# Moving the start addresses of the matmul operands of a two-layer decoder trunk

## The chip, the cores and the metric
The kernel runs on one core of a Trainium2 chip. The metric is device time in microseconds, the median of three runs; the profiler adds one profiled execution, whose span goes from its first to its last instruction.

## The reference
The program computes a decoder trunk of two layers for 256 tokens of 2048 features in float32. Layer 0 mixes tokens with a sparse attention of three branches, layer 1 with a matrix memory (mLSTM); after each mixer stands a gated feed-forward network with a short convolution. All large products have the form `xn @ w`:

```
x = x + nsa_mixer(rms_norm(x, g0), ...)          # xn @ w_in (2048 x 3632), o @ w_out (2048 x 2048)
x = x + conv_glu_ffn(rms_norm(x, g1), ...)       # u = xn @ w_up (2048 x 11264); conv; silu(gate)*val @ w_down (5632 x 2048)
x = x + mlstm_mixer(rms_norm(x, g2), ...)        # xn @ w_in (2048 x 6160), h @ w_out (2048 x 2048)
x = x + conv_glu_ffn(rms_norm(x, g3), ...)
return rms_norm(x, norm_final)
```

## The kernel before, in words
Precision comes from splitting. Every operand is held as a high half, rounded to the format `float32r` that TensorE takes, and a low half, the rest; a product is three matmuls into one PSUM bank: high by high, high by low, low by high. The activations are `xh` and `xl`, laid out with features on the partitions. Weights come from memory as `raw` (SyncE's queue, 512 KB a piece, four buffers); ACT copies `raw` to `whi` (line 189), DVE subtracts to `wlo` (line 191), five buffers each; TensorE then takes them.

A matmul has a stationary operand, which a weight load (PEld) brings in, and a moving operand, which is streamed. There are two forms.

The columns form (`cols_piece`, lines 225 to 228) is used for the attention's compressed keys and values, keys and queries, for the mLSTM's queries and keys and for the whole up projections. The weights are stationary (128 x 128), the 256 tokens of `xh` or `xl` are moving. A piece is 4 feature tiles x 2 column tiles x 3 matmuls = 24 matmuls; the three are (whi, xh), (whi, xl), (wlo, xh), stationary operand first.

The rows form (`rows_mm`, lines 197 to 199) has the activations stationary and the weights moving. Its order is (high, whi), (high, wlo), (low, whi). It serves two uses: the projections of `xh`/`xl` that are wanted with tokens on partitions (`rows_times`, 256 to 512 columns), and all output projections (`project_out`, 512 columns and in the very last two banks 256), where the stationary operand is a stage's own output: `oh`/`ol` in the attention, `moh`/`mol` in the mLSTM, `gh`/`gl` in the feed-forward network.

The order of the work is the order in which the program issues it: side work (attention, mLSTM heads, norms) is handed out between pieces from a queue (`tick`), and evacuations of PSUM banks follow each product.

Tiles are placed one behind the other within a pool, and pools one behind the other, in the order of allocation. What a tile takes on each partition is its number of elements times 4 bytes, rounded up to 32. Added up from the start, that gives each tile's start address; its remainder modulo 256 is called its phase here. All large tiles are multiples of 256 bytes long, as are the steps between buffers, feature tiles and 128-column blocks, so a phase holds for every buffer and nearly every block of a tile; the exceptions are the widths 412, 416 and 304 of `rows_times`, whose second and third blocks begin inside a tile at another phase. Unused pad tiles (`pad_w`, `pad_x`, `pad_m`, `pad_f`) set the phases. Before, they are: `xh` and `xl` 96; `raw`, `whi`, `wlo` 32; `gh`, `gl`, `oh`, `ol`, `moh`, `mol` 32.

Of the kernel before, what the change touches and what calls it, by code (L numbers as in the profile page):

```python
# [12 lines left out]
F32 = mybir.dt.float32  # L13
# [8 lines left out]
P = 128  # L22
# [40 lines left out]
def trunk(ctx: ExitStack, tc: tile.TileContext, x, positions, nsa_w_in, nsa_gate_b, nsa_cmp_pe,  # L63
# [8 lines left out]
    const = ctx.enter_context(tc.tile_pool(name="const", bufs=1))  # L72
    main = ctx.enter_context(tc.tile_pool(name="main", bufs=1))
    wpool = ctx.enter_context(tc.tile_pool(name="wpool", bufs=1))
    wpool.tile([P, 48], F32, name="pad_w")
    small = ctx.enter_context(tc.tile_pool(name="small", bufs=2))
    psum = ctx.enter_context(tc.tile_pool(name="psum", bufs=8, space=PSUM))

# [2 lines left out]
    def nm(s):  # L81
        uid[0] += 1
        return f"{s}_{uid[0]}"
# [4 lines left out]
    def fview(t):  # L88
        return t.bitcast(F32)

    h = main.tile([P, NT, D], F32, name="h")
    main.tile([P, 16], F32, name="pad_x")
    xh = main.tile([P, KT, S], F32R, name="xh")
    xl = main.tile([P, KT, S], F32R, name="xl")

# [75 lines left out]
    def queued(engine):  # L171
        return tc.issue_after(fence[engine]) if engine in fence else nullcontext()
# [3 lines left out]
    def preload(w, k0, nk, c0, n):  # L176
        ready[w.tensor.name, w.offset, k0, c0] = load_split(w, k0, nk, c0, n)

    def load_split(w, k0, nk, c0, n):
        got = ready.pop((w.tensor.name, w.offset, k0, c0), None)  # L180
        if got is not None:
            return got
        view = lambda t: t[:, :nk * n].rearrange("p (k c) -> p k c", k=nk)
        raw = wpool.tile([P, 1024], F32, name=nm("raw"), tag="raw", bufs=RAWB)
        nc.sync.dma_start(view(raw), w[k0 * P:(k0 + nk) * P, c0:c0 + n].rearrange("(k p) c -> p k c", p=P))
        hi = wpool.tile([P, 1024], F32R, name=nm("whi"), tag="whi", bufs=SPB)
        lo = wpool.tile([P, 1024], F32R, name=nm("wlo"), tag="wlo", bufs=SPB)
        with queued("act"):
            latest["act"] = act(view(hi), view(raw), AF.Copy).ins  # L189
        with queued("ve"):  # L190
            latest["ve"] = ve.tensor_sub(view(lo), view(raw), fview(view(hi))).ins  # L191
        return view(hi), view(lo)
# [8 lines left out]
    def rows_times(w, c0, n, nk):  # L201
        accs = [bank() for _ in range(NT)]
        for k0 in range(0, KT, nk):
            m = min(nk, KT - k0)
            hi, lo = load_split(w, k0, m, c0, n)
            run_hooks()
            for i in range(m):
                kt = k0 + i
                for t in range(NT):
                    rows_mm(hi, lo, i, xh, xl, kt, t, accs[t][:, :n], 0, n, kt == 0, kt == KT - 1)  # L210
            tick()
        return accs
# [4 lines left out]
    def cols_piece(ps, w, c0, k0, n):  # L217
        hi, lo = load_split(w, k0, n, c0, 256)
        run_hooks()
        for i in range(n):  # L220
            for j in range(2):
                kt = k0 + i
                a = hi[:, i, j * P:(j + 1) * P]
                b = lo[:, i, j * P:(j + 1) * P]
                mm(ps[:, j, :], a, xh[:, kt, :], start=(kt == 0 and j == 0), stop=False,  # L225
                   skip_group_check=True)
                mm(ps[:, j, :], a, xl[:, kt, :], start=False, stop=False, skip_group_check=True)  # L227
                mm(ps[:, j, :], b, xh[:, kt, :], start=False, stop=(kt == KT - 1 and j == 1),  # L228
                   skip_group_check=True)
        tick()  # L230

    def cols_times(w, c0):
        ps = pair_bank()
        for k0 in range(0, KT, 4):
            cols_piece(ps, w, c0, k0, 4)
        return ps
# [109 lines left out]
    def nsa(norm, nxt):  # L346
        with tc.tile_pool(name="nsa", bufs=1) as pool, tc.tile_pool(name="nsw", bufs=2) as wk:
# [18 lines left out]
            pct = pool.tile([80, 512], F32R, name="pct")  # L366
            nc.gpsimd.memset(fview(vcmp), 0.0)
            nc.gpsimd.memset(fview(pct), 0.0)
            oh = pool.tile([P, HEADS, S], F32R, name="oh")
            ol = pool.tile([P, HEADS, S], F32R, name="ol")  # L370

            nc.gpsimd.dma_start(per, nsa_cmp_pe[0].rearrange("c l d -> l c d"))
# [303 lines left out]
    def mlstm(norm, nxt):  # L676
        with tc.tile_pool(name="mls", bufs=1) as pool, tc.tile_pool(name="mlw", bufs=2) as wk:
# [4 lines left out]
            sog = pool.tile([P, NT, D], F32, name="sog")  # L682
            v1 = pool.tile([P, NT, MH, DV + 1], F32, name="v1")
            nc.gpsimd.memset(v1[:, :, :, DV:DV + 1], 1.0)
            pool.tile([P, 16], F32, name="pad_m")
            oh = pool.tile([P, KT, S], F32R, name="moh")
            ol = pool.tile([P, KT, S], F32R, name="mol")
            gp = pool.tile([P, NT, 2 * MH], F32, name="gp")
            li, lf, u, w1p, bcol, ecol = (pool.tile([P, NT, MH], F32, name=n)
# [163 lines left out]

    def ffn(layer, norm, nxt):
        with tc.tile_pool(name=f"ffn{layer}", bufs=1) as pool, tc.tile_pool(name=f"ffw{layer}", bufs=2) as wk:
            pool.tile([P, 48], F32, name=f"pad_f{layer}")
            wu, wd = ffn_w_up[layer], ffn_w_down[layer]
            taps = tapc[:, layer]

            def conv(ff, tag, ps):  # L860
                uu = wk.tile([P, 2, S], F32, name=nm("u"), tag="u" + tag)
                ve.tensor_mul(uu, ps, norm.rbc2)  # L862
                ac = wk.tile([P, 2, S], F32, name=nm("ac"), tag="ac" + tag)
                for j in range(2):
                    f = ff + j
                    act(ac[:, j, :], uu[:, j, :], AF.Identity, bias=taps[:, 3, f:f + 1],  # L866
                        scale=taps[:, 2, f:f + 1])
                    ve.scalar_tensor_tensor(ac[:, j, 1:], uu[:, j, :S - 1], taps[:, 1, f:f + 1],  # L868
                                            ac[:, j, 1:], op0=ALU.mult, op1=ALU.add)
                    ve.scalar_tensor_tensor(ac[:, j, 2:], uu[:, j, :S - 2], taps[:, 0, f:f + 1],  # L870
                                            ac[:, j, 2:], op0=ALU.mult, op1=ALU.add)
                return ac

            groups = [list(range(0, 4))] + [list(range(f, f + 8)) for f in range(4, NFF, 8)]

            def up(ffs):
                gh = wk.tile([P, 8, S], F32R, name=nm("gh"), tag="gh")
                gl = wk.tile([P, 8, S], F32R, name=nm("gl"), tag="gl")
                for i in range(0, len(ffs), 2):
                    res = {}  # L880

                    def gate_out(ff, ps, res):
                        res["g"] = conv(ff, "g", ps)
                        act(res["g"], res["g"], AF.Silu)

                    def val_out(ff, ps, res, i):
                        va = conv(NFF + ff, "v", ps)
                        ve.tensor_mul(va, res["g"], va)
                        act(gh[:, i:i + 2, :], va, AF.Copy)
                        ve.tensor_sub(gl[:, i:i + 2, :], va, fview(gh[:, i:i + 2, :]))  # L890

                    evacs.append(partial(gate_out, ffs[i], cols_times(wu, ffs[i] * P), res))
                    evacs.append(partial(val_out, ffs[i], cols_times(wu, (NFF + ffs[i]) * P), res, i))
                return gh, gl

            def down(ffs, g, norm):
                n = len(ffs)
                project_out(wd[ffs[0] * P:(ffs[0] + n) * P, :], g[0], g[1], n, norm)

            prev = None  # L900
            for ffs in groups:
                g = up(ffs)
                if prev is not None:
                    down(*prev, None)
                prev = (ffs, g)
            down(*prev, nxt)
# [60 lines left out]
    after(8, partial(measure, 1))  # L967
    after(12, n0.settle)
    nsa(n0, n1)
    ffn(0, n1, n2)  # L970
    mlstm(n2, n3)
    nf.load()
    ffn(1, n3, nf)


# [21 lines left out]
```

## Time and profile before

| | us |
|---|---|
| median of 3 runs | 2221.46 (2220.2 to 2222.11) |
| the profiled execution's own time | 2222.36 |
| span of the profiled execution | 2220.6 |
| TensorE busy (99%) | 2203.8 |
| DVE busy (65%) | 1444.2 |
| ACT busy (50%) | 1113.4 |

A busy time is the sum of the stretches in which an engine has an instruction under way; matmuls overlap each other, so a matmul's own duration is longer than the distance to the next one. The distance is read from starts: in the timeline, or in the view of one source line, which gives a line's first and last start and how many there are. PE is TensorE's matmuls, PEld its weight loads. Names after `<-` are the operands.

### The profile page before, as it was taken

The page shows a single profiled execution, that of the slowest core. Times are in us where ns is not written, and L with a number is a line of the kernel's source. Part 1 is how long each engine was busy: PE and PEld are TensorE (multiplying, and loading weights), DVE is VectorE, ACT ScalarE, POOL GpSimd, SP SyncE. Part 2 cuts the span into 40 slices and gives each one's busy share as a digit, 9 for nine tenths or more (in the row PEclk, how much of TensorE's full clock was granted, in tenths as well). Part 3 has the DMA queues.
Part 4 walks back from the last instruction along what each step waited for, and adds up shares of the span by engine and source line. Part 5 has one row for each costly group of instructions (what it writes and reads, how often), then busy time and mean ns, then how long its engine had stood idle before and what let it go on. Part 6 is the DMA issues. An engine that isn't in the chain of part 4 may idle for free.

```text
span 2220.6 us, 37284 instructions
## 1 busy us (share of the span) xinstructions
PE 2203.8 (99%) x15072; PEld 2042.1 (92%) x15072; DVE 1444.2 (65%) x2191; ACT 1113.4 (50%) x1565; POOL 19.1 (1%) x56
## 2 busy tenths in 40 slices
PE   9999999999999999999999999999999999999998
PEld 8899789999999899998899988899999899998987
DVE  6488757676656666665645665667666566675755
ACT  6366655554445454454654444555545454454544
POOL 2000000000000000000000000000000000000000
PEclk9999999999999999999999999999999999999999
DMA  8653355666666666666567655566666666666664
GB/s 242 204 166 106 112 162 180 189 183 190 188 191 189 191 187 186 192 187 191 165 187 200 171 171 167 169 197 191 188 191 184 193 185 189 190 187 192 184 195 133
DMA packets 298317, 403.33 MB, mean 182 GB/s; under 512 B 12904, under 2 KB 256840, under 8 KB 298016
## 3 DMA queue, kind: packets, MB, share of 16 engines
q1 hardware_dynamic: 297264, 399.03, 59.6%
q8 instruction: 118, 1.93, 0.4%
q0 software_dynamic: 688, 1.83, 0.3%
q14 instruction: 55, 0.45, 0.1%
q10 hardware_dynamic: 192, 0.08, 0.0%
HBM read 398.80 MB, written 2.10 MB: 181 GB/s over the span
## 4 chain that ended last, share of the span: by engine, by line
PE 97%; DMA 1%; ACT 1%; DVE 1%; issue 0%; SPq 0%; ACTq 0%
PE bank L225 18%; PE bank L228 18%; PE bank L227 18%; PE bank L197 13%; PE bank L199 13%; PE bank L198 13%; DMA raw<-in_nsa_w_in_dram 1%; PE bank L548 1%; PE bank L259 1%; PE bank L579 0%; DMA h<-in_x_dram 0%; ACT whi L189 0%; ACT pr L552 0%; PE bank L523 0%; DVE wlo L191 0%; PE bank L597 0%
## 5 line engine op out<-in xcount | busy, mean ns | idle before, releaser
L191 DVE TENSOR_TENSOR wlo<-raw,whi 128x1024 fp32r<-128x1024 f32 (+3 forms) x755 | 912.6, 1210 | 609.8 <-ACT whi L189 607.4
L189 ACT ACTIVATE whi<-raw 128x1024 fp32r<-128x1024 f32 (+3 forms) x755 | 790.4, 1048 | 955.3 <-PE bank L227 483.5
L225 PE MATMUL bank<-xh,whi 128*128 128x256 f32 x3456 | 970.4, 281 | 3.2 <-ACT whi L189 2.6
L228 PE MATMUL bank<-xh,wlo 128*128 128x256 f32 x3456 | 965.8, 280 | 1.5 <-DVE wlo L191 1.5
L227 PE MATMUL bank<-xl,whi 128*128 128x256 f32 x3456 | 965.4, 279 | 0.1
L225 PEld LDWEIGHTS bank<-xh,whi 128*128 128x128 f32 x3456 | 649.1, 188 | 7.7 <-ACT whi L189 3.4
L228 PEld LDWEIGHTS bank<-xh,wlo 128*128 128x128 f32 x3456 | 650.1, 188 | 1.9 <-DVE wlo L191 1.9
L227 PEld LDWEIGHTS bank<-xl,whi 128*128 128x128 f32 x3456 | 648.2, 188 | 1.3 <-DVE xl L265 0.4
L197 PE MATMUL bank<-whi,gh 128*128 128x512 f32 (+1 forms) x712 | 276.1, 388 | 0.0
L199 PE MATMUL bank<-whi,gl 128*128 128x512 f32 (+1 forms) x712 | 275.5, 387 | 0.0
L198 PE MATMUL bank<-wlo,gh 128*128 128x512 f32 (+1 forms) x712 | 275.3, 387 | 0.0
L199 PEld LDWEIGHTS bank<-whi,gl 128*128 128x128 f32 x712 | 133.7, 188 | 27.4
L198 PEld LDWEIGHTS bank<-wlo,gh 128*128 128x128 f32 x712 | 133.8, 188 | 26.8
L197 PEld LDWEIGHTS bank<-whi,gh 128*128 128x128 f32 x712 | 133.7, 188 | 26.5
L197 PE MATMUL bank<-whi,xh 128*128 128x412 f32 (+4 forms) x352 | 128.0, 364 | 0.0
L199 PE MATMUL bank<-whi,xl 128*128 128x412 f32 (+4 forms) x352 | 125.2, 356 | 0.0
L198 PE MATMUL bank<-wlo,xh 128*128 128x412 f32 (+4 forms) x352 | 125.1, 355 | 0.0
L866 ACT ACTIVATE ac<-u,tapc 128x256 f32<-128x256 f32 x176 | 95.0, 587 | 3.8 <-DVE u L862 3.8
L310 DVE TENSOR_TENSOR h<-bank,h 128x512 f32<-128x512 f32 (+1 forms) x113 | 72.9, 682 | 34.5 <-PE bank L199 34.3
L862 DVE TENSOR_TENSOR u<-bank,rbc 128x512 f32<-128x512 f32 x88 | 60.8, 691 | 52.8 <-PE bank L228 52.8
L868 DVE SCALAR_TENSOR_TENSOR ac<-u,tapc,ac 128x255 f32<-128x255 f32 x176 | 77.3, 479 | 3.0 <-ACT ac L866 3.0
L870 DVE SCALAR_TENSOR_TENSOR ac<-u,tapc,ac 128x254 f32<-128x254 f32 x176 | 77.2, 479 | 0.3
(251 smaller groups left out, 1505.6 us busy)
## 6 DMA issues: line engine op xcount, KB each, us to landing
raw<-in_ffn_w_up_dram SPq DMA_DIRECT2D x352, 512.0 KB, 3.7
raw<-in_ffn_w_down_dram SPq DMA_DIRECT2D x176, 512.0 KB, 4.4
raw<-in_mlstm_w_in_dram SPq DMA_DIRECT2D x64, 512.0 KB, 3.8
raw<-in_nsa_w_in_dram SPq DMA_DIRECT2D x51, 512.0 KB, 4.6
raw<-in_nsa_w_out_dram SPq DMA_DIRECT2D x32, 512.0 KB, 3.7
raw<-in_mlstm_w_out_dram SPq DMA_DIRECT2D x32, 512.0 KB, 4.4
raw<-in_mlstm_w_in_dram SPq DMA_DIRECT2D x32, 412.0 KB, 4.1
raw<-in_nsa_cmp_w_dram SPq DMA_DIRECT2D x16, 256.0 KB, 3.4
```

The lines of the kernel that those rows point to most:

```text
L189: latest["act"] = act(view(hi), view(raw), AF.Copy).ins
L191: latest["ve"] = ve.tensor_sub(view(lo), view(raw), fview(view(hi))).ins
L197: mm(o, a, hi[:, i, c:e], start=first, stop=False)
L198: mm(o, a, lo[:, i, c:e], start=False, stop=False)
L199: mm(o, b, hi[:, i, c:e], start=False, stop=last)
L225: mm(ps[:, j, :], a, xh[:, kt, :], start=(kt == 0 and j == 0), stop=False, skip_group_check=True)
L227: mm(ps[:, j, :], a, xl[:, kt, :], start=False, stop=False, skip_group_check=True)
L228: mm(ps[:, j, :], b, xh[:, kt, :], start=False, stop=(kt == KT - 1 and j == 1), skip_group_check=True)
L310: ve.tensor_add(h[:, t, a:b], acc[:, :b - a], h[:, t, a:b])
L866: act(ac[:, j, :], uu[:, j, :], AF.Identity, bias=taps[:, 3, f:f + 1], scale=taps[:, 2, f:f + 1])
L868: ve.scalar_tensor_tensor(ac[:, j, 1:], uu[:, j, :S - 1], taps[:, 1, f:f + 1], ac[:, j, 1:], op0=ALU.mult, op1=ALU.add)
L870: ve.scalar_tensor_tensor(ac[:, j, 2:], uu[:, j, :S - 2], taps[:, 0, f:f + 1], ac[:, j, 2:], op0=ALU.mult, op1=ALU.add)
```

## The change
The change touches pad tiles alone: two are made smaller, one larger, one is taken away and five are added. `pad_w` goes from 48 to 16 words and `pad_x` goes; a pad of 32 words (128 bytes) is put between the `whi` and the `wlo` buffers, before `oh` and before `ol`, between `moh` and `mol`, and between the `gh` and the `gl` buffers; `pad_m` grows from 16 to 48 words and `pad_f` shrinks from 48 to 16. No instruction, operand shape, order or buffer count is altered. Added up in the same way, the phases become:

| tiles | before | after |
|---|---|---|
| xh, xl | 96 | 32 |
| raw, whi | 32 | 96 |
| wlo | 32 | 224 |
| gh, oh, moh | 32 | 96 |
| gl, ol, mol | 32 | 224 |

```diff
-    wpool.tile([P, 48], F32, name="pad_w")
+    wpool.tile([P, 16], F32, name="pad_w")
...
-    main.tile([P, 16], F32, name="pad_x")
...
+    apart = []
+
     def load_split(w, k0, nk, c0, n):
...
         hi = wpool.tile([P, 1024], F32R, name=nm("whi"), tag="whi", bufs=SPB)
+        if not apart:
+            apart.append(wpool.tile([P, 32], F32, name="pad_lo"))
         lo = wpool.tile([P, 1024], F32R, name=nm("wlo"), tag="wlo", bufs=SPB)
...
+            pool.tile([P, 32], F32, name="pad_oh")
             oh = pool.tile([P, HEADS, S], F32R, name="oh")
+            pool.tile([P, 32], F32, name="pad_ol")
             ol = pool.tile([P, HEADS, S], F32R, name="ol")
...
-            pool.tile([P, 16], F32, name="pad_m")
+            pool.tile([P, 48], F32, name="pad_m")
             oh = pool.tile([P, KT, S], F32R, name="moh")
+            pool.tile([P, 32], F32, name="pad_n")
             ol = pool.tile([P, KT, S], F32R, name="mol")
...
-            pool.tile([P, 48], F32, name=f"pad_f{layer}")
+            pool.tile([P, 16], F32, name=f"pad_f{layer}")
+            pads = []
...
                 gh = wk.tile([P, 8, S], F32R, name=nm("gh"), tag="gh")
+                if not pads:
+                    pads.append(wk.tile([P, 32], F32, name=f"pad_g{layer}", tag="pad_g", bufs=1))
                 gl = wk.tile([P, 8, S], F32R, name=nm("gl"), tag="gl")
```

## Rows read from the trace of the kernel before

**Rows 1.** The page, busy shares and 40 slices: TensorE and its granted clock in tenths.
```profile
PE 2203.8 (99%) x15072; PEld 2042.1 (92%) x15072; DVE 1444.2 (65%) x2191; ACT 1113.4 (50%) x1565; POOL 19.1 (1%) x56
...
PE   9999999999999999999999999999999999999998
...
PEclk9999999999999999999999999999999999999999
```
**Rows 2.** The page's chain by engine and line; then TensorE's waits, us, times, longest.
```profile
PE 97%; DMA 1%; ACT 1%; DVE 1%; issue 0%; SPq 0%; ACTq 0%
PE bank L225 18%; PE bank L228 18%; PE bank L227 18%; PE bank L197 13%; PE bank L199 13%; PE bank L198 13%; DMA raw<-in_nsa_w_in_dram 1%; PE bank L548 1%; PE bank L259 1%; PE bank L579 0%; DMA h<-in_x_dram 0%; ACT whi L189 0%; ACT pr L552 0
...
PE bank L225 <- ACT whi L189: 2.6, 2, 1.8
PE bank L228 <- DVE wlo L191: 1.5, 2, 0.8
```
**Rows 3.** Timeline, up projection of layer 0: start us, us, engine, line, operands.
```profile
699.87 0.28 PE L225 MATMUL bank<-xh,whi 128*128 128x256 f32 x1
699.87 0.19 PEld L227 LDWEIGHTS bank<-xl,whi 128*128 128x128 f32 x1
699.99 0.28 PE L227 MATMUL bank<-xl,whi 128*128 128x256 f32 x1
```
**Rows 4.** Groups by line and shape, TensorE: xcount | busy us, mean ns | idle before.
```profile
L225 PE MATMUL bank<-xh,whi 128*128 128x256 f32 x3456 | 970.4, 281 | 3.2 <-ACT whi L189 2.6 <-ACT xh L264 0.6
...
L197 PE MATMUL bank<-whi,gh 128*128 128x512 f32 x696 | 271.6, 390 | 0.0
...
L197 PE MATMUL bank<-whi,xh 128*128 128x512 f32 x128 | 52.7, 411 | 0.0
L197 PE MATMUL bank<-whi,moh 128*128 128x512 f32 x128 | 51.2, 400 | 0.0
L197 PE MATMUL bank<-whi,oh 128*128 128x512 f32 x128 | 51.0, 399 | 0.0
...
L197 PE MATMUL bank<-whi,xh 128*128 128x412 f32 x128 | 44.5, 348 | 0.0
```
**Rows 5.** Line 225 in one up projection: count, durations, first and last start.
```profile
L225 PE MATMUL bank<-xh,whi x256: 280/280/282, 640.2 to 730.3; 128*128 128x256 f32 x128
```
**Rows 6.** Line 197 in one down projection, in the same form.
```profile
L197 PE MATMUL bank<-whi,gh x64: 389/389/402, 864.6 to 907.5; 128*128 128x512 f32 x64
```
**Rows 7.** Timeline, one query piece during the attention; 21 starts lie between.
```profile
166.54 0.28 PE L227 MATMUL bank<-xl,whi 128*128 128x256 f32 x1
...
168.92 0.28 PE L227 MATMUL bank<-xl,whi 128*128 128x256 f32 x1
```
**Rows 8.** Timeline, NSA value columns, xh stationary; 20, then 14 starts apart.
```profile
37.84 0.28 PE L197 MATMUL bank<-whi,xh 128*128 128x256 f32 x1
...
40.19 0.28 PE L199 MATMUL bank<-whi,xl 128*128 128x256 f32 x1
...
44.41 0.28 PE L197 MATMUL bank<-whi,xh 128*128 128x256 f32 x1
...
46.00 0.28 PE L199 MATMUL bank<-whi,xl 128*128 128x256 f32 x1
```
**Rows 9.** Timeline, end of the last down projection, 256 columns; 24 starts apart.
```profile
2208.56 0.28 PE L199 MATMUL bank<-whi,gl 128*128 128x256 f32 x1
...
2211.44 0.28 PE L199 MATMUL bank<-whi,gl 128*128 128x256 f32 x1
```
**Rows 10.** Timeline, mLSTM value columns, xh stationary, 512 columns; 12 starts apart.
```profile
1228.22 0.39 PE L197 MATMUL bank<-whi,xh 128*128 128x512 f32 x1
...
1231.02 0.39 PE L197 MATMUL bank<-whi,xh 128*128 128x512 f32 x1
```
**Rows 11.** The page's costliest groups, DVE and ACT: busy, mean ns | idle, releaser.
```profile
L191 DVE TENSOR_TENSOR wlo<-raw,whi 128x1024 fp32r<-128x1024 f32 (+3 forms) x755 | 912.6, 1210 | 609.8 <-ACT whi L189 607.4
L189 ACT ACTIVATE whi<-raw 128x1024 fp32r<-128x1024 f32 (+3 forms) x755 | 790.4, 1048 | 955.3 <-PE bank L227 483.5
```
**Rows 12.** The page's DMA issues of weights: count, KB each, us to landing.
```profile
raw<-in_ffn_w_up_dram SPq DMA_DIRECT2D x352, 512.0 KB, 3.7
...
raw<-in_nsa_w_in_dram SPq DMA_DIRECT2D x51, 512.0 KB, 4.6
```

## The prediction

> **What bounds the kernel now.** I read the busy shares and slices first, then the chain of waits, then what TensorE waits for, then the matmuls by shape, and last single stretches of the timeline. TensorE is busy in every slice at full granted clock (the 2.4 GHz level) [rows 1]; the chain that ends last lies 97% on it, nearly all in the six matmul lines L225, L227, L228, L197, L198, L199, and what TensorE waits for most in the whole run is 2.6 us of weights [rows 2]. So no wait is left to remove. The time is the number of matmuls times their pitch, the distance from one start to the next, and only a change of pitch can move it. The "mean ns" of a matmul is no pitch, since neighbours overlap: in the columns stage each is drawn 0.28 us long and the next starts 0.12 us later, and the weight load of the next matmul starts together with the current matmul [rows 3]. That order matters here: while matmul i streams its moving operand, the stationary operand of matmul i+1 is read.
>
> Two stages carry the time. The columns stage (weights stationary, xh or xl moving, 256 columns) has 3 x 3456 = 10368 matmuls [rows 4]. Its pitch is (730.3 - 640.2)/765 = 117.8 ns: 256 instances of L225 from first to last start, three matmuls each [rows 5]. That is 1221 us, 55% of the span. The rows stage over gh, oh and moh (weights moving, 512 columns) has 3 x (696 + 128 + 128) = 2856 [rows 4], at (907.5 - 864.6)/189 = 227.0 ns [rows 6], so 648 us. The third kind, xh or xl stationary with 512, 416, 412, 304 or 256 columns, is small: 3 x 128 = 384 of 512 columns, as many of 412 [rows 4], and 96 of each other width.
>
> **The change, part by part.** No instruction, transfer or wait is added or removed. The pads move start addresses. What one can sensibly compare is the offset between the operand streaming in matmul i and the stationary operand being read for i+1, modulo 256 bytes. In the columns stage the order is (whi, xh), (whi, xl), (wlo, xh), so the pairs are xh with whi, xl with wlo, xh with whi. Before: 96 - 32 = +64 in all three. After: 32 - 96 = -64, then 32 - 224 = -192 = +64, then -64. In the rows stage over gh, oh, moh the pairs are whi with gh, wlo with gl, whi with gh: 0 before, and 96 - 96 and 224 - 224 = 0 after. In the rows stage over xh the pairs have 32 - 96 = -64 before and +64, -64, +64 after.
>
> Now the pitch by offset, as far as this trace shows it. With 256 columns, +64: 117.8 ns almost everywhere; in one single piece of the attention stretch, (168.92 - 166.54)/21 = 113.3 ns [rows 7]. With 256 columns and -64 (the NSA value columns, xh stationary): (40.19 - 37.84)/20 = 117.5 ns, and after a disturbance in its third piece (46.00 - 44.41)/14 = 113.6 ns until the piece ends [rows 8]. With 256 columns and 0 (the end of the last down projection): (2211.44 - 2208.56)/24 = 120.0 ns [rows 9]. With 512 columns, 0: 227.0 [rows 6]; -64: (1231.02 - 1228.22)/12 = 233.3 ns [rows 10]. So start addresses do matter: the same matmul of 512 columns costs 6.3 ns more at one offset. And a pitch is a state into which the two reads lock: one address pattern has two, 113.3 and 117.8.
>
> *Columns stage.* Both signs of 64 give 117.5 to 117.8 ns in their usual state, and after the change every pair has one of the two. No row shows a sequence that alternates. Bounds: 113.3 ns, 10368 x 4.5 = 47 us less; 120.0 ns, 10368 x 2.2 = 23 us more. I take 117.8 and no change, being nearest to rows with both signs, and keep both ends.
>
> *Rows stage over gh, oh, moh.* The offset stays 0, so 227.0 ns and no change. Unlike before, streams of phase 96 and 224 follow one another; no row shows such a change, so I bound it by the spread of the 512-column pitches, 6.3 ns either way: 2856 x 6.3 = 18 us. I take 0.
>
> *Rows stage over xh, 512 columns.* Two of three pairs leave the offset at which 233.3 was seen. What +64 costs with 512 columns is not shown; between 227.0 and 233.3 I take the middle, 3.2 ns on 384 matmuls, a gain of 1.2 us, with ends 2.4 us and none. The 412, 416, 304 and 256 widths (384 + 3 x 96 = 672 matmuls) start at mixed phases already, since their second and third pieces begin inside a tile; at 6.3 ns they are good for 4 us either way, taken as 0.
>
> *The other engines.* ACT writes whi and DVE writes wlo at new phases. DVE's subtraction takes 1210 ns and ACT's copy 1048 ns on average, 755 of each, and both wait most for TensorE or for one another [rows 11]; were each 100 ns slower, 76 us more busy time would still lie under a TensorE that waits for them 4.1 us in total [rows 2]. The 512 KB weight transfers land in 3.7 to 4.6 us [rows 12] into buffers four deep; the raw buffers move by 64 bytes and keep that cover. If the cover went, a late copy would appear as a wait of L225 for L189. Cost 0.
>
> The Trainium skill, page "SBUF — State Buffer", section "Who interferes with whom", speaks against any effect: it says that TensorE reads the moving and the stationary operand through two independent ports and waits for nobody. By it every phase would cost the same. The rows above disagree with it for this kernel, 227.0 against 233.3 ns [rows 6, 10], so I do not treat it as settled.
>
> *Sum.* The profiled execution took 2222.36 us, 1.8 more than its span of 2220.6. Less 1.2 gives 2221.2. That execution lies 0.9 us above the median of the three runs, 2221.46, so 2220 us is forecast for the median. Its own range is 2216 to 2225: the 4 us of the odd widths.
>
> **The rivals.**
> *The columns stage locks into the fast state* (faster). For it: the 113.3 ns state exists at both signs [rows 7, 8], and at -64, which two of three pairs now have, one piece of four reached it, against one of 432 (10368/24) at +64. Against it: before, the state was left at every interruption. All of it gives 2221.5 - 47 = 2174 us. A partial form, one or two of the three matmuls or a share of the pieces, gives 2190 to 2212.
>
> *The alternation breaks the lock* (slower). The mechanism: in the columns stage all three reads now sit at one offset, so whatever delay a collision brings is the same each time and both reads settle with it; -64, +64, -64 shifts the next read by 128 bytes after each matmul, and a group pays a fresh collision. It decides from the point where that costs over 0.4 ns per matmul (4.4 us in 10368). Nearest price: the pitch at the offset 0, 120.0 ns, so 2221.5 + 23 = 2244 us; two such steps would make 2267. For it: 6.3 to 6.7 ns steps are what these rows show a collision to cost. Against it: no row alternates.
>
> *Phases are no lever at all* (the change does nothing): what differs between rows 6 and 10 is then the stage, not the address. Same shape, same operations, so weak; 2221.5 us. This is also what the Trainium skill's rule of the independent ports gives.
>
> **How the numbers follow.** Unchanged columns stage, with the small gain or with none: 0.36 (0.26 for the forecast, 0.10 for phases as no lever). Faster columns or rows stage: 0.41, of which 0.18 all of it, 0.20 partial, 0.03 beyond 47 us through the 512-column rows as well. Slower: 0.23, of which 0.16 up to 23 us and 0.07 beyond. This kernel's measurement can tell about 0.2%, 4.4 us, from no change. So faster 0.41, same 0.36, slower 0.23. The largest single case is the forecast with its neighbour, hence 2220 us; the range from 2173 to 2246 us leaves out 0.03 below and 0.07 above, and since both signs hold much of the chance the forecast's own 2216 to 2225 stands beside it.
>
> **What would show it.** In the changed kernel's profile, the starts of L225 in an up projection: still 117.8 ns apart is the forecast, 113.3 the first rival, 120 or more the second. L197 in a down projection: 227.0 ns. L197 with xh at 512 columns: under 233.3. L189, L191 and the waits of TensorE: as before. The prediction is wrong if the columns pitch moves by more than 0.4 ns, or if TensorE's waits for weights grow from 4 us to tens.

## The result, and the profile after

The changed kernel takes 2189.32 us (median of 4 runs, 2188.51 to 2189.75), the one before 2221.67 in the same series (4 runs, 2220.2 to 2222.11): a ratio of 0.9855, 95% interval 0.9843 to 0.9867. It is faster by 32 us. The forecast was 2220 us; the time lies between the first rival's 2174 us (all matmuls of the columns stage at 113.3 ns) and the 2190 us at which its partial form begins.

The page of the changed kernel, in the order of [rows 1], [rows 2] and [rows 11] (its lines are three higher: L228, L230, L231 are the columns stage, L200 to L202 the rows stage):

```profile
PE 2170.5 (99%) x15072; PEld 1999.7 (91%) x15072; DVE 1441.2 (66%) x2191; ACT 1114.1 (51%) x1565; POOL 19.2 (1%) x56
...
PEclk9999999999999999999999999999999999999999
...
PE 97%; ACT 1%; DVE 1%; DMA 1%; issue 0%; SPq 0%; ACTq 0%
...
L194 DVE TENSOR_TENSOR wlo<-raw,whi 128x1024 fp32r<-128x1024 f32 (+3 forms) x755 | 911.8, 1209 | 591.7 <-ACT whi L192 590.6
L192 ACT ACTIVATE whi<-raw 128x1024 fp32r<-128x1024 f32 (+3 forms) x755 | 791.2, 1049 | 913.7 <-PE bank L230 429.1
```

What TensorE waits for most in the changed kernel (us in all, times, longest):

```profile
PE bank L228 <- ACT whi L192: 1.9, 2, 1.2
PE bank L231 <- DVE wlo L194: 1.5, 2, 0.8
```

What differs here from before is the busy time of TensorE, 33 us less in matmuls and 42 us less in weight loads, for the same 15072 of each. The granted clock is 0.996 of full speed, against 0.999: from 86.3 to 89.7 us it stands at its lower level (1.2 GHz), behind two waits of TensorE for weights of 1.21 and 0.76 us, and 16 matmuls at some 0.21 us cost about 1.6 us there. ACT and DVE take the same time at the new phases, and the waits are as small. So the pitch has moved, and the views of one line show where. The up and the down projection of a layer take turns in parts; a stretch is one such part. First line 228 in a stretch of an up projection and line 200 in one of a down projection of the changed kernel, to be held against [rows 5] and [rows 6]:

```profile
L228 PE MATMUL bank<-xh,whi x251: 276/276/279, 633.2 to 718.2; 128*128 128x256 f32 x126
...
L200 PE MATMUL bank<-whi,gh x63: 387/392/398, 850.4 to 893.4; 128*128 128x512 f32 x63
```

The columns stage now runs at 85.0/750 = 113.3 ns (117.8 before), and the rows stage at 43.0/186 = 231.2 ns (227.0 before). The first got faster, the second slower. For the whole run I summed the distances from each matmul's start to the next one's over the trace, by stage (the 10.5 us that are missing to the span lie ahead of the first matmul and behind the last start):

| us | columns | rows over gh, oh, moh | rows over xh | the rest | span |
|---|---|---|---|---|---|
| before | 1229.5 | 657.8 | 207.4 | 115.4 | 2220.6 |
| after | 1188.1 | 668.9 | 206.3 | 114.2 | 2188.0 |
| difference | -41.4 | +11.1 | -1.1 | -1.2 | -32.6 |

A fast columns pitch is entered, not given. The timeline of the changed kernel at the entry of a stretch of up projection, line 228 alone, three matmuls from row to row and fifteen to the last row:

```profile
500.34 0.28 PE L228 MATMUL bank<-xh,whi 128*128 128x256 f32 x1
...
500.69 0.28 PE L228 MATMUL bank<-xh,whi 128*128 128x256 f32 x1
...
501.05 0.28 PE L228 MATMUL bank<-xh,whi 128*128 128x256 f32 x1
...
501.40 0.28 PE L228 MATMUL bank<-xh,whi 128*128 128x256 f32 x1
...
501.76 0.28 PE L228 MATMUL bank<-xh,whi 128*128 128x256 f32 x1
...
502.10 0.28 PE L228 MATMUL bank<-xh,whi 128*128 128x256 f32 x1
...
503.80 0.28 PE L228 MATMUL bank<-xh,whi 128*128 128x256 f32 x1
```

The first four steps take 1.42 us, 118.3 ns a matmul; from there five groups take 1.70 us, 113.3 ns, and so it stays to the end of the stretch. Over the run I counted groups of three matmuls, each from one start of (whi, xh) to the next within a stretch, by a third of that distance; of the 3399 groups those from 112 to 115.5 ns are called fast, those from 115.5 to 119 slow. Before, 6 groups are fast, 3347 slow and 13 lie between 119 and 121 ns; after, 3256, 49 and 54. What is left, 33 and 40 groups, is longer and lies at entries and interruptions and, after, in the stretch at the lower clock.

### The profile page after: what moved, and what is told of

Same layout as the page of the kernel before. It is cut to its first block, busy times and chain, and to the rows that moved or that the text cites. A ratio compares the mean times of both kernels' runs of the same rounds, so it can differ in the third digit from the quotient of the medians.

```text
span 2188.0 us, 37284 instructions
## 1 busy us (share of the span) xinstructions
PE 2170.5 (99%) x15072; PEld 1999.7 (91%) x15072; DVE 1441.2 (66%) x2191; ACT 1114.1 (51%) x1565; POOL 19.2 (1%) x56
## 4 chain that ended last, share of the span: by engine, by line
PE 97%; ACT 1%; DVE 1%; DMA 1%; issue 0%; SPq 0%; ACTq 0%
PE bank L228 18%; PE bank L231 18%; PE bank L230 18%; PE bank L201 13%; PE bank L200 13%; PE bank L202 13%; PE bank L553 1%; PE bank L262 1%; ACT pr L557 0%; ACT whi L192 0%; PE bank L584 0%; DVE wlo L194 0%; DMA h<-in_x_dram 0%; PE bank L528 0%; DMA raw<-in_nsa_w_in_dram 0%; PE bank L602 0%
## 5 line engine op out<-in xcount | busy, mean ns | idle before, releaser
L194 DVE TENSOR_TENSOR wlo<-raw,whi 128x1024 fp32r<-128x1024 f32 (+3 forms) x755 | 911.8, 1209 | 591.7 <-ACT whi L192 590.6
L192 ACT ACTIVATE whi<-raw 128x1024 fp32r<-128x1024 f32 (+3 forms) x755 | 791.2, 1049 | 913.7 <-PE bank L230 429.1
L228 PE MATMUL bank<-xh,whi 128*128 128x256 f32 x3456 | 959.3, 278 | 3.1 <-ACT whi L192 1.9
L231 PE MATMUL bank<-xh,wlo 128*128 128x256 f32 x3456 | 956.1, 277 | 1.5 <-DVE wlo L194 1.5
L230 PE MATMUL bank<-xl,whi 128*128 128x256 f32 x3456 | 956.3, 277 | 0.2 <-DVE xl L268 0.2
L228 PEld LDWEIGHTS bank<-xh,whi 128*128 128x128 f32 x3456 | 650.4, 188 | 7.6 <-ACT whi L192 2.8
L231 PEld LDWEIGHTS bank<-xh,wlo 128*128 128x128 f32 x3456 | 650.4, 188 | 1.9 <-DVE wlo L194 1.9
L230 PEld LDWEIGHTS bank<-xl,whi 128*128 128x128 f32 x3456 | 650.5, 188 | 1.4 <-DVE xl L268 0.5
L201 PE MATMUL bank<-wlo,gh 128*128 128x512 f32 (+1 forms) x712 | 279.8, 393 | 0.0
L200 PE MATMUL bank<-whi,gh 128*128 128x512 f32 (+1 forms) x712 | 278.1, 391 | 0.0
L202 PE MATMUL bank<-whi,gl 128*128 128x512 f32 (+1 forms) x712 | 277.1, 389 | 0.0
L200 PEld LDWEIGHTS bank<-whi,gh 128*128 128x128 f32 x712 | 133.9, 188 | 30.9
L202 PEld LDWEIGHTS bank<-whi,gl 128*128 128x128 f32 x712 | 133.7, 188 | 30.0
L200 PE MATMUL bank<-whi,xh 128*128 128x412 f32 (+4 forms) x352 | 128.2, 364 | 0.0
L202 PE MATMUL bank<-whi,xl 128*128 128x412 f32 (+4 forms) x352 | 124.8, 354 | 0.0
```

The source lines that it names most:

```text
L200: mm(o, a, hi[:, i, c:e], start=first, stop=False)
L201: mm(o, a, lo[:, i, c:e], start=False, stop=False)
L202: mm(o, b, hi[:, i, c:e], start=False, stop=last)
```

## The experiments

**Theories.** A, the alternation: what matters is that successive reads differ by 128 bytes. B, the sign: a moving operand 64 bytes below the stationary one that is read beside it makes the fast pitch, one 64 above the slow one. C, the pair: the pitch follows from the offsets of the pairs alone (moving in matmul i, stationary for i+1), -64, +64, -64, however they come about. D, the absolute address: the position within a piece of 64 bytes counts, so that phases 32 and 96 differ from 64 and 128. The rows of a down projection were followed beside it. "Phases x, hi/lo, out/out" below are the bytes modulo 256 of the activations, of the high and low halves of the weights, and of the high and low halves of the outputs that the rows stage holds stationary; before is 96, 32/32, 32/32, after is 32, 96/224, 96/224.

**e1, one phase (32, 96/96, 96/96): the sign without the alternation.** Against the kernel before:

```diff
-    wpool.tile([P, 48], F32, name="pad_w")
+    wpool.tile([P, 16], F32, name="pad_w")
...
-    main.tile([P, 16], F32, name="pad_x")
```

> Activations at 32; raw, whi, wlo and all stationary outputs at 96, high and low alike. In the columns stage the offset is then -64 in all three pairs; in the rows stage over gh, oh, moh it is 0 and all phases are equal. Theory A (the alternation -64, +64, -64 puts the columns stage into its fast state): alternation is gone, columns pitch back to 117.8 ns, rows 227.0 ns, total near 2220 us. Theory B (the sign: -64 for the high halves does it): columns stay at 113.3 ns, rows 227.0 ns, total near 2221.5 - 10368 x 4.4 ns = 2176 us, faster than the changed kernel.

2207.24 us, ratio 0.9934 (0.9919 to 0.9949). Two stretches of the up projection of layer 0 in this kernel (count, durations, first and last start):

```profile
L224 PE MATMUL bank<-xh,whi x334: 276/276/276, 363.7 to 476.9; 128*128 128x256 f32 x167
...
L224 PE MATMUL bank<-xh,whi x255: 281/281/281, 633.3 to 723.1; 128*128 128x256 f32 x128
```

The first runs at 113.2/999 = 113.3 ns from end to end, the second at 89.8/762 = 117.8. No long stretch mixes them: the pitch is settled at the entry and held for 90 to 114 us, while ACT and DVE go on beside it. Which one it is goes by the place: of the ten long stretches the first of each layer's up projection (1008 matmuls) is fast in both layers, and the eight (768 matmuls) that follow directly on a part of the down projection are slow. In all 1102 groups of three run fast and 2263 slow. So the sign makes the fast pitch reachable and does not secure it, and neither of the two totals expected came: by the sum of distances the columns take 1214.4 us, 15.1 less than before, where the changed kernel gains 41.4. B explains a good third of the gain in the columns stage. Rows stage: 226.5 ns (42.8/189), as before.

**e2, low halves apart with the sign of before (96, 32/160, 32/160): the alternation without the sign.** Against the changed kernel:

```diff
-    wpool.tile([P, 16], F32, name="pad_w")
+    wpool.tile([P, 48], F32, name="pad_w")
...
+    main.tile([P, 16], F32, name="pad_x")
```

> Activations at 96 and high halves at 32 as before the change, low halves 128 bytes apart (160), stationary outputs 32 and 160. Columns offsets +64, -64, +64, the mirror of the changed kernel; rows 0 with moving phases 32, 160, 32. Theory A (alternation): columns at 113.3 ns, rows at the 230 to 233 ns of the changed kernel, total near 2189 us. Theory B (sign of the high halves' offset): columns 117.8 ns, rows 230 to 233, total near 2189 + 46 = 2235 us.

2219.19 us, 1.0025 (0.999 to 1.006). Its executions fall into two groups with nothing between, 2217.0 to 2219.8 (six) and 2240.6 to 2243.6 (four), at granted clocks of 0.997 to 0.999 in both; the profiled one, 2241.06, is of the second, so the median and the ratio stand for neither group. One stretch of up projection of the profiled one, and a short one of the mLSTM's queries and keys:

```profile
L229 PE MATMUL bank<-xh,whi x256: 278/279/280, 643.9 to 734.8; 128*128 128x256 f32 x128
...
L229 PE MATMUL bank<-xh,whi x48: 276/276/363, 1319.1 to 1335.2; 128*128 128x256 f32 x48
```

The first runs at 90.9/765 = 118.8 ns, and so do all ten long stretches: groups at 117.8 and at 120.0 ns follow one another by turns, that is, every second group takes 6.7 ns more. The short one runs at 113.3 ns behind its first group. In all 110 groups are fast, 1636 slow and 1619 between 119 and 121. By the sums of distances the columns take 1238.9 us, 9.4 more than before, and the rows over outputs 668.7, 10.9 more. So A alone is refuted: the alternation with the other sign does not secure the fast pitch, and in this execution it makes the columns slower. The six quicker executions left no trace. If their rows cost the same, their columns take some 1216 us (an estimate: 1238.9 less the 23 us between the groups), less than before; so this run does not show that the alternation with this sign is always worse. The second rival's price, a step of 6.3 to 6.7 ns, is seen here, in every second group; that it is a collision of two reads is not shown.

**e3, low outputs back (32, 96/224, 96/96): does the lower offset matter in the rows stage?** Against the changed kernel:

```diff
-            pool.tile([P, 32], F32, name="pad_ol")
...
-            pool.tile([P, 32], F32, name="pad_n")
...
-                if not pads:
-                    pads.append(wk.tile([P, 32], F32, name=f"pad_g{layer}", tag="pad_g", bufs=1))
```

> The changed kernel with gl, ol and mol at 96 like their high halves: the pads before them are taken out. Columns stage untouched: 113.3 ns by every theory. Rows over gh, oh, moh: offsets 0, +128, 0 in place of 0, 0, 0, with moving phases still 96, 224, 96. If the rows stage became slower because the moving phase changes from matmul to matmul, it stays at 230 to 233 ns and the total at 2189 us; if it depends on the offset alone, the pair of wlo and gl gets a new price, between 220 and 240 ns on 952 matmuls, total 2179 to 2196 us.

2193.57 us, 0.9873 (0.9859 to 0.9888). A stretch of down projection, at 44.1/189 = 233.3 ns:

```profile
L200 PE MATMUL bank<-whi,gh x64: 393/397/398, 850.2 to 894.3; 128*128 128x512 f32 x64
```

Columns as in the changed kernel (3290 fast groups); the rows stage costs 674.0 us by the sum of distances, 5 more than after and 16 more than before. The pads on the outputs' low halves do help, but only against a loss that the change itself makes: the low halves of the weights, moving at 224 among high halves moving at 96 (e9 below tests this).

**e4, all phases 32 bytes on (64, 128/0, 128/0).** One pad of 8 words ahead of everything:

```diff
+    main.tile([P, 8], F32, name="pad_x")
     xh = main.tile([P, KT, S], F32R, name="xh")
```

> The changed kernel with 32 bytes more before xh, so that every phase behind it moves by 32 (activations 64, high 128, low 0) and every offset stays. Theory C (only offsets between the two reads matter): nothing changes, 2189 us. Theory D (memory is read in pieces of 64 bytes, 16 columns of 4 bytes, at 6.67 ns each: the fast state of 113.3 ns is 17 pieces for 256 columns that start in the middle of a piece): 16 pieces do, the columns pitch falls to 106.7 to 109 ns and the 512-column pitch by 6.7 ns; 2189 - 10368 x 4.3 to 6.7 ns - 3240 x 6.7 ns = about 2100 to 2125 us.

2188.27 us, 0.9849 (0.9833 to 0.9866), the changed kernel's time; one stretch of up projection of it:

```profile
L229 PE MATMUL bank<-xh,whi x249: 276/276/276, 632.9 to 717.2; 128*128 128x256 f32 x125
```

84.3/744 = 113.3 ns. D is refuted at this step: at a shift of 32 bytes only the differences count.

**e5, the same pairs made by the moving operands (xh 32, xl 160, 96/96, 96/96).** The pairs in the columns stage are again -64, +64, -64, but now the moving operand alternates and the stationary one does not. Against e1:

```diff
-    wpool.tile([P, 16], F32, name="pad_w")
+    wpool.tile([P, 48], F32, name="pad_w")
...
     xh = main.tile([P, KT, S], F32R, name="xh")
+    main.tile([P, 32], F32, name="pad_xl")
     xl = main.tile([P, KT, S], F32R, name="xl")
```

> xh at 32, xl at 160; raw, whi, wlo and all stationary outputs at 96. Columns offsets -64, +64, -64 as in the changed kernel, but now the moving operand alternates and the weights' phases are all one; rows over gh, oh, moh: offset 0 with one phase everywhere, as before the change. Theory of offsets (what counts is the offset between the operand streaming in matmul i and the one loaded for i+1): columns 113.3 ns nearly everywhere, rows 227.0 ns, total 2189 less the 231.4 - 227.0 = 4.4 ns on 2856 row matmuls, near 2177 us. Rival (the phases of successive weight loads, or of the writes of whi and wlo, count): columns as with one phase for both halves of the weights, 117.1 ns on average, total near 2207 us.

2220.05 us, 0.9994 (0.9985 to 1.0004). A stretch of up and one of down projection:

```profile
L225 PE MATMUL bank<-xh,whi x256: 277/280/282, 638.2 to 728.3; 128*128 128x256 f32 x128
...
L197 PE MATMUL bank<-whi,gh x64: 388/390/390, 728.7 to 771.5; 128*128 128x512 f32 x64
```

90.1/765 = 117.8 ns, and over the run 3 groups are fast and 3344 slow. Neither of the expected totals, 2177 and 2207 us, came. C, on which the prediction's whole table of offsets rests, is refuted: the same pairs give 113.3 or 117.8. It is not saved by pairing a moving operand with the stationary one of its own matmul, or of the one after the next: the three offsets of either kernel are then the same again, in rotated order. Against e1, moving xl away from xh takes away even the third that was fast.

**e6, e7, e8: other offsets in the rows stage.** e5 with the outputs at 224/224, 32/160 and 160/32, by pads ahead of them (e7's and e8's have other sizes and one each ahead of ol, mol and gl):

```diff
+            pool.tile([P, 32], F32, name="pad_oh")
...
-            pool.tile([P, 16], F32, name="pad_m")
+            pool.tile([P, 48], F32, name="pad_m")
...
-            pool.tile([P, 48], F32, name=f"pad_f{layer}")
+            pool.tile([P, 16], F32, name=f"pad_f{layer}")
```

> The kernel with xh 32, xl 160, weights 96, and all stationary outputs at 224: rows over gh, oh, moh at offset 96 - 224 = 128 in all pairs; columns as with the outputs at 96. If the rows stage is governed by the offset as the columns stage is, its pitch leaves 227.0 ns: down to 220 ns (the 16 cycles over the column count that the fast columns state shows), 20 us less, or up to 240 ns, 37 us more than with the outputs at 96. If offset 0 and 128 are alike, 227 ns.

> The kernel with xh 32, xl 160, weights 96, and outputs' high halves at 32, low halves at 160: rows offsets +64, -64, +64. If the alternation helps rows as it helps columns, one of this and its mirror image reaches 220 ns, 20 us less than with offset 0; by the 512-column product over xh, which has these offsets in the changed kernel, 230 ns, 9 us more.

> The kernel with xh 32, xl 160, weights 96, and outputs' high halves at 160, low halves at 32: rows offsets -64, +64, -64, the very offsets at which the columns stage is fast. If what is good for 256 columns is good for 512, 220 ns and 20 us less than with offset 0; if the number of columns decides which offset is good, 227 to 236 ns, up to 26 us more.

2235.68 (1.0064, 1.0044 to 1.0084), 2226.63 (1.0023, 1.0012 to 1.0033) and 2233.08 us (1.0049, 1.0033 to 1.0065). A stretch of down projection of e6, then of e7, then of e8:

```profile
L197 PE MATMUL bank<-whi,gh x64: 390/393/404, 734.5 to 778.4; 128*128 128x512 f32 x64
```
```profile
L197 PE MATMUL bank<-whi,gh x64: 393/394/395, 730.9 to 774.2; 128*128 128x512 f32 x64
```
```profile
L197 PE MATMUL bank<-whi,gh x64: 392/393/395, 733.0 to 776.8; 128*128 128x512 f32 x64
```

232.3, 229.1 and 231.7 ns. No offset tried betters the 227.0 of [rows 6] and the 226.5 of e5 (42.8/189), both with moving and stationary operand at one phase throughout.

**e9, two views: low halves at 224 where they are stationary, at 96 where they move (32, 96 with 224 or 96, 96/96).** The buffers of the low halves get 32 words more, so that a view can begin at either phase; as the buffers are now 4224 bytes long, their own phases are 96 and 224 by turns, and the view starts at 0 or 32 words by the buffer's number and the use. The mask mt_b goes into the mLSTM's own pool for room. Against e3, the main lines:

```diff
-    def load_split(w, k0, nk, c0, n):
+    lows = [0]
+
+    def load_split(w, k0, nk, c0, n, cols=False):
...
-        if not apart:
-            apart.append(wpool.tile([P, 32], F32, name="pad_lo"))
-        lo = wpool.tile([P, 1024], F32R, name=nm("wlo"), tag="wlo", bufs=SPB)
+        lo = wpool.tile([P, 1056], F32R, name=nm("wlo"), tag="wlo", bufs=SPB)
+        at = 32 * ((lows[0] % SPB + cols) % 2)
+        lows[0] -= 1
+        lo = lo[:, at:at + 1024]
```

> The changed kernel, but each wlo buffer is 128 bytes longer and the low halves are put at 224 where they are stationary (columns) and at 96 where they move (rows); gl, ol, mol at 96. Columns as in the changed kernel, rows with one phase everywhere, as before the change. If the loss of the rows stage comes from the low halves' moving phase, rows return to 227.0 ns while columns stay at 113.3 ns: 2189 - 2856 x 4.4 ns = about 2177 us, faster than both kernels. If the fast columns state needs the low halves to be written or kept at 224 throughout, columns go back toward 117 ns and the total to 2200 us or more.

2177.20 us (5 runs, 2176.27 to 2178.91), 0.9802 (0.9789 to 0.9815): 12 us below the changed kernel and 44 below the one before, the best of all versions here, and the time that was expected. A stretch of up projection and the one of down projection behind it:

```profile
L226 PE MATMUL bank<-xh,whi x253: 276/276/276, 629.4 to 715.1; 128*128 128x256 f32 x127
...
L198 PE MATMUL bank<-whi,gh x64: 389/389/393, 715.8 to 758.6; 128*128 128x512 f32 x64
```

85.7/756 = 113.4 and 42.8/189 = 226.5 ns. By the sums of distances the columns take 1185.2 us and the rows over outputs 657.6, 16 less than in e3. Both halves of the reading hold together: the columns want the low halves 128 bytes apart, the rows want them where the high halves are.

**e10 and e11: is it 128, or any difference?** e3 with the low halves 64 bytes off, at 160 and at 32 (the pad of 32 words ahead of wlo becomes 16, or 48; pads behind it keep the outputs at 96):

```diff
-            apart.append(wpool.tile([P, 32], F32, name="pad_lo"))
+            apart.append(wpool.tile([P, 16], F32, name="pad_lo"))
```

> Activations 32, high halves and all stationary outputs 96, low halves of the weights 160 in place of 224. Columns offsets -64, -128, -64. If any difference between the high and the low halves keeps the columns stage from staying in the slow state, 113.3 ns and a total near the 2194 us of the same kernel with 224; if the 128 bytes between the halves matter, columns go to 117 ns or above, a total of 2205 to 2240 us.

> Activations 32, high halves and all stationary outputs 96, low halves of the weights 32. Columns offsets -64, 0, -64. If any difference between the halves will do, 113.3 ns and near 2194 us; if the offset 0 in one pair of three costs what it costs at 256 columns in all three (120.0 ns), columns 115.5 to 120 ns and 2215 to 2260 us.

2238.95 (1.0079, 1.0061 to 1.0098) and 2228.21 us (1.003, 1.0015 to 1.0044). A stretch of up projection of e10, then of e11:

```profile
L228 PE MATMUL bank<-xh,whi x251: 279/283/286, 643.6 to 732.3; 128*128 128x256 f32 x126
```
```profile
L228 PE MATMUL bank<-xh,whi x243: 275/281/281, 642.5 to 728.0; 128*128 128x256 f32 x122
```

118.3 and 117.8 ns in these stretches and over the run: both lose the fast pitch, with 3 and 10 fast groups left. Of the four differences tried, with activations 64 below the high halves, 128 secures it, 0 gives it in a third of the groups, 64 either way takes it away. The rows pay for any difference: with all outputs at 96 and the low halves moving at 96, 32, 160 and 224 they take 657.6 (e9), 663.4 (e11), 670.9 (e10) and 674.0 us (e3).

## Why the prediction was right in part and missed the time

*What bounds the kernel.* Right: matmuls times pitch. The span fell by 32.6 us with the count and the waits unchanged, and the clock no higher. The range of 2173 to 2246 us holds the measured 2189, but it is as wide as the rivals together, and that it holds says little; the forecast's own 2216 to 2225 does not hold it.

*Columns stage.* This step failed. It took "117.8 and no change" because both signs of 64 stood near 117.8 in their usual state; measured are 113.3 ns in 3256 of 3399 groups, 41.4 us less, where all 10368 matmuls at the lower pitch would have given the 47 us of the bound. The rest is some 100 slow groups behind entries (about 2 us), the 1.6 us at the lower clock, and interruptions. By its own sign, a columns pitch that moves by more than 0.4 ns, the prediction was wrong here. The two levels were read rightly from the rows, as states that last (that it is the reads that lock is not shown); what was wrong was to take a state's frequency before as its frequency under a sequence that no row showed. The first rival had the outcome, the columns stage at 113.3 ns, and its evidence, one piece in four at -64 against one in 432 at +64 [rows 7, 8], pointed the right way: e1, with -64 alone, is fast in a third of its groups. What it lacked is that the 128 bytes between high and low halves are what makes the pitch of 113.3 ns all but certain.

*The measure behind it.* The offset of the pairs was taken to decide the pitch. e5 shows that it does not: the same pairs by another route give 117.8. It matters which operand alternates.

*Rows stage over gh, oh, moh.* "Offset 0, so 227.0 ns and no change" failed as well: 231.2 ns, 11.1 us more, inside the bound of 18 us but not zero. e5 and e9 give 226.5 with both halves moving at one phase; the changed kernel keeps the offset 0 and loses 4 ns. The term that was left at nothing, streams of phase 96 and 224 following one another, is the cost: between e3 and e9, with the outputs at 96 in both, it is 16.4 us.

*Rows stage over xh.* Right, and small: forecast 1.2 us less, measured 1.1. With 512 columns these matmuls took 91.8 us before and take 90.8 after; the pitch is 231.7 ns between two starts of line 200 that lie six matmuls apart:

```profile
1212.87 0.39 PE L200 MATMUL bank<-whi,xh 128*128 128x512 f32 x1
...
1214.26 0.39 PE L200 MATMUL bank<-whi,xh 128*128 128x512 f32 x1
```

*The other engines.* Right: DVE 1209 ns and ACT 1049, TensorE's waits for them 1.9 and 1.5 us.

*The other rivals.* "The alternation breaks the lock" did not hold for this pattern. Of its neighbours e5 and e11 stay at the 117.8 ns of before, and e2 (its profiled execution) and e10 go above it, to 118.8 and 118.3 ns, not to the 120.0 of the rival. "Phases are no lever" is refuted by e1 alone, where one pad less and one shorter take 14 us off. The Trainium skill, page "SBUF — State Buffer", section "Who interferes with whom", says that TensorE waits on nobody there; as far as it is read to mean that start addresses don't matter, these runs disagree, from 2177.20 us (e9) to 2238.95 (e10) with the same matmuls.

What stays open: why stationary operands 128 bytes apart dislodge the pitch of 117.8 ns, and moving operands 128 bytes apart do the opposite. The trace has starts and ends of instructions, and no view of it shows the single reads, so the runs give the pattern and not its cause. In every run the phase at which DVE writes a low half is also the one at which TensorE reads it, so they do not tell which of the two counts; nor why an entry in e1 settles at one pitch or the other. Other sets of phases than those listed were not tried.

## What to carry to other kernels

Where TensorE is busy from end to end and waits for nothing, measure the pitch, start to start, of each stage, and look whether one line shows two pitches at one clock: that is time which start addresses may move, as they did here. Try phases in runs, with each stage's pitch read by itself, since one tile can be stationary in one stage and moving in another and want a different address in each. A pitch that occurs rarely before says little on how often it will occur under a new sequence: give it its own weight in the forecast.

## What the runs showed of the hardware that was not expected

- One kernel, one program, two pitches: in e1 whole stretches of 90 to 114 us run at 113.3 or at 117.8 ns, settled at their entry, and the same stretches of both layers at the same one.
- e2 shows the same between executions: 2217.0 to 2219.8 or 2240.6 to 2243.6 us, with 21 us and nothing between.
- A shift of all operands by 32 bytes changes nothing (e4, 2188.27 against 2189.32 us), one of the low halves alone by 64 costs 35 and 45 us (e11 and e10 against e3).
- The drawn duration of a matmul of 256 columns tells the fast pitch too: its median is 276 ns at 113.3, and 279 to 283 in the stretches shown at 117.8 to 118.8.
